# Down projection of the channel mixer: three groups of k tiles by Strassen's seven products, two weight sums made by loads that accumulate

## The chip, the cores and the metric

One core of one Trainium2 chip. The metric is the device time of one execution in microseconds (us), the median over runs. Engines: PE (TensorE, matrix products; PEld is its weight load), DVE (VectorE), ACT (ScalarE), POOL (GpSimd), SP (SyncE, which here only issues transfers). Each engine has its own queue and runs it in order; between engines there are semaphores.

## The reference

Four layers over 512 tokens of 1024 channels in float32. Each layer is a token mixer (convolution module, 2-D neighbourhood attention, bidirectional retention, convolution module again), then a channel mixer. Each of the two reads the RMS-normed residual and adds its result to it.

```python
for i in range(DEPTH):                       # 4
    ...                                      # token mixer, x = x + y
    h = rmsnorm(x, norm2_g[i])
    x = x + conv_ffn(h, ffn_w_up[i], ffn_dw_w[i], ffn_dw_b[i], ffn_w_down[i])
```

`conv_ffn` multiplies by `w_up` (1024 x 5632), applies a depthwise convolution of width 3 over the tokens, takes the tanh form of gelu of one half times the other half (2816 hidden channels), and multiplies by `w_down` (2816 x 1024). The change concerns this last product.

## The kernel before

Everything lies transposed: channels on the 128 partitions, 512 tokens (T) in the free dimension. The residual is eight tiles x0 to x7. A float32 product is made of three products in the faster float32r form: every operand is split into a rounded high half and a low half (the difference), and `mm3` (L161 to L164) issues hi x hi, hi x lo and lo x hi into the same PSUM bank. A weight tile arrives by one load on SP's queue into `wr` (two buffers of 1024 columns); ACT casts it to `wh` (L157), DVE subtracts to get `wl` (L158). Three buffers each of `wh` and `wl` let the split run ahead of PE.

`ffn(l, after)` runs the channel mixer of layer l. `up(n)` makes one of 44 column blocks of the up projection (8 input tiles x 3 products of 128x512). `mid(j)` takes two of those, applies the convolution and the gate (DVE L298, L303, L305, L309; ACT L301, L308), and splits the result into `hh` and `hl` (L172, L173), for 22 hidden tiles j. Then a loop over the eight output tiles o loads three pieces of weights (1024, 896, 896 columns), runs 22 k tiles x 3 products of 128x512 into one bank, adds the bank to x[o] (`residual`, L274), and calls `after(o)`. In layers 0 to 2 `after(o)` is `prep` of the next stage: `xh` (ACT L229), `xl` (DVE L232), a square (ACT L245) and its addition to `sqacc` (POOL L250). In layer 3 it is the store of x[o] (L1044); there the last output tile is made in two token halves with an addition (L362) and a store each.

The order on each engine is made by the Tile scheduler from the program's order, its priorities and its own model of durations; the kernel does not write it out.

## Time and profile before

| what | value |
|---|---|
| median of 3 runs | 2581.75 us (2581.56 to 2582.65) |
| profiled execution: span from first to last instruction | 2576.2 us, the time of that execution as the profile has it |
| granted TensorE clock | 1.000 |
| PE rows in the program's order | 13168 |

A row of the timeline reads: start in us, length in us, engine, line, operation, out<-in, shapes, and in brackets the idle time before it with what ended it. A row by groups reads: line, engine, operation, out<-in, shapes, count, then busy us and mean ns of one, then idle time before it and what ended it. In the row on a window of time the engines stand in the order PE, PEld, DVE, ACT, POOL with their busy us, then the granted clock, the DMA engines' busy share and GB/s. A row of transfers has the issuing queue (SPq, POOLq), the count, KB each, and the median us from issue to landing.

### The profile page before, as it was taken

What the parts mean: (1) busy time and instruction counts of PE and PEld (TensorE: products, weight loads), DVE (VectorE), ACT (ScalarE), POOL (GpSimd) and SP (SyncE); (2) the same over time, 40 slices, a digit from 0 to 9 for tenths busy, and PEclk for the clock granted to TensorE, in tenths of its full rate; (3) what the DMA queues carried; (4) which work ended last, traced back from release to release, by engine and by line L of the source; (5) the groups of instructions that cost most, each with busy time, mean ns of one, the idle gap of its engine ahead of it and who ended that gap; (6) DMA issues with size and microseconds to landing.
All of it is one profiled execution on the core that took longest, in us unless ns stands there. A gap on an engine that the chain in (4) does not pass through costs nothing.

```text
span 2576.2 us, 33719 instructions
## 1 busy us (share of the span) xinstructions
PE 2558.8 (99%) x13414; PEld 2120.2 (82%) x13414; DVE 1652.3 (64%) x2673; ACT 1050.0 (41%) x1439; POOL 258.8 (10%) x301
## 2 busy tenths in 40 slices
PE   9999999999999999999999999999999999999999
PEld 7878888889998888888888888888888888788888
DVE  7986777338877777624656566677743787677732
ACT  5554444335556444423333323444432445444421
POOL 1213000003421100000000000100000221100000
PEclk9999999999999999999999999999999999999999
DMA  6724232333332322233222221232333672222232
GB/s 241 234 86 148 90 98 88 95 103 105 97 91 71 101 95 95 90 97 110 74 85 71 84 80 58 98 99 90 97 90 97 206 222 74 90 93 95 92 107 80
DMA packets 80174, 271.78 MB, mean 105 GB/s; under 512 B 10720, under 2 KB 13664, under 8 KB 80016
## 3 DMA queue, kind: packets, MB, share of 16 engines
q1 hardware_dynamic: 73152, 256.32, 30.9%
q0 software_dynamic: 5568, 10.59, 1.7%
q10 hardware_dynamic: 1296, 2.72, 0.3%
q8 instruction: 105, 1.72, 0.3%
q14 instruction: 53, 0.43, 0.1%
HBM read 260.19 MB, written 5.63 MB: 103 GB/s over the span
## 4 chain that ended last, share of the span: by engine, by line
PE 97%; DVE 2%; ACT 0%; issue 0%; DMA 0%; SPq 0%; DVEq 0%; ACTq 0%
PE ps L164 27%; PE ps L163 27%; PE ps L162 27%; PE ps L168 3%; PE ps L169 3%; PE ps L167 3%; PE ps L485 1%; PE ps L484 1%; PE ps L483 1%; PE ps L332 1%; PE ps L333 1%; PE ps L337 1%; PE ps L724 1%; DMA x<-in_xT 0%; PE ps L539 0%
## 5 line engine op out<-in xcount | busy, mean ns | idle before, releaser
L157 ACT CAST wh<-wr 128x1024 fp32r<-128x1024 f32 (+1 forms) x410 | 423.1, 1033 | 1086.1 <-PE ps L163 775.9
L164 PE MATMUL ps<-xh,wl 128*128 128x512 f32 x1856 | 735.4, 397 | 0.1
L163 PE MATMUL ps<-xl,wh 128*128 128x512 f32 x1856 | 734.5, 396 | 0.2 <-DVE xl L232 0.2
L162 PE MATMUL ps<-xh,wh 128*128 128x512 f32 x1856 | 730.4, 394 | 0.4 <-ACT wh L157 0.4
L158 DVE TENSOR_TENSOR wl<-wr,wh 128x1024 fp32r<-128x1024 f32 (+1 forms) x407 | 494.9, 1216 | 334.4 <-ACT wh L157 332.1
L162 PEld LDWEIGHTS ps<-xh,wh 128*128 128x128 f32 x1856 | 348.5, 188 | 85.8 <-ACT wh L157 1.3
L163 PEld LDWEIGHTS ps<-xl,wh 128*128 128x128 f32 x1856 | 348.4, 188 | 85.9 <-DVE xl L232 0.5
L164 PEld LDWEIGHTS ps<-xh,wl 128*128 128x128 f32 x1856 | 348.3, 188 | 81.7 <-DVE wl L158 0.5
L162 PE MATMUL ps<-hh,wh 128*128 128x512 f32 (+1 forms) x726 | 281.6, 388 | 0.5 <-DVE x L362 0.5
L163 PE MATMUL ps<-hl,wh 128*128 128x512 f32 (+1 forms) x726 | 281.5, 388 | 0.0
L164 PE MATMUL ps<-hh,wl 128*128 128x512 f32 (+1 forms) x726 | 281.5, 388 | 0.0
L298 DVE TENSOR_TENSOR t<-ps,rstd_bc 128x512 f32<-128x512 f32 x176 | 120.8, 690 | 159.1 <-PE ps L164 159.1
L250 POOL TENSOR_TENSOR sqacc<-t,sqacc 128x512 f32<-128x512 f32 x49 | 75.1, 1533 | 1253.6 <-ACT t L245 1248.2
L162 PEld LDWEIGHTS ps<-hh,wh 128*128 128x128 f32 x726 | 136.6, 188 | 31.0 <-DVE x L362 0.7
L163 PEld LDWEIGHTS ps<-hl,wh 128*128 128x128 f32 x726 | 136.7, 188 | 30.3
L164 PEld LDWEIGHTS ps<-hh,wl 128*128 128x128 f32 x726 | 136.7, 188 | 30.3
L168 PE MATMUL ps<-wl,xh 128*128 128x256 f32 (+1 forms) x512 | 159.1, 312 | 0.5 <-DVE wl L158 0.5
L169 PE MATMUL ps<-wh,xl 128*128 128x256 f32 (+1 forms) x512 | 159.1, 312 | 0.0
L167 PE MATMUL ps<-wh,xh 128*128 128x256 f32 (+1 forms) x512 | 158.4, 312 | 0.0
L301 ACT ACTIVATE t<-t,par 128x512 f32<-128x512 f32 x176 | 142.5, 814 | 6.0 <-DVE t L298 5.8
L305 DVE SCALAR_TENSOR_TENSOR t<-t,par,t 128x511 f32<-128x511 f32 x176 | 132.0, 750 | 5.5
L303 DVE SCALAR_TENSOR_TENSOR t<-t,par,t 128x511 f32<-128x511 f32 x176 | 130.8, 744 | 0.0
(256 smaller groups left out, 3572.4 us busy)
## 6 DMA issues: line engine op xcount, KB each, us to landing
wr<-in_f_up SPq DMA_DIRECT2D x176, 512.0 KB, 3.4
wraw<-in_cdw SPq DMA_DIRECT2D x56, 608.0 KB, 5.1
wr<-in_f_down SPq DMA_DIRECT2D x64, 448.0 KB, 3.3
wr<-in_f_down SPq DMA_DIRECT2D x32, 512.0 KB, 3.5
wr<-in_cw_in SPq DMA_DIRECT2D x30, 512.0 KB, 3.9
wr<-in_nat_qkv SPq DMA_DIRECT2D x24, 512.0 KB, 3.5
wr<-in_cw_out SPq DMA_DIRECT2D x16, 512.0 KB, 3.9
wr<-in_ret_qk SPq DMA_DIRECT2D x16, 512.0 KB, 3.5
```

The costliest lines, as they stand in the source:

```text
L157: nc.scalar.copy(hi[:, :n], raw[:, :n])
L158: eng.tensor_tensor(lo[:, :n], raw[:, :n], hi[:, :n].bitcast(F32), SUB)
L162: nc.tensor.matmul(o, wh, ah, start=first, stop=False)
L163: nc.tensor.matmul(o, wh, al, start=False, stop=False)
L164: nc.tensor.matmul(o, wl, ah, start=False, stop=last)
L167: nc.tensor.matmul(o, ah, wh, start=first, stop=False)
L168: nc.tensor.matmul(o, ah, wl, start=False, stop=False)
L169: nc.tensor.matmul(o, al, wh, start=False, stop=last)
L298: nc.vector.tensor_tensor(u, ps, rstd_bc, MUL)
L301: nc.scalar.activation(a, u, AF.Identity, bias=pc("fdb", l * 44 + c), scale=pt[:, w + 1:w + 2])
L303: nc.vector.scalar_tensor_tensor(a[:, 1:], u[:, :T - 1], pt[:, w:w + 1], a[:, 1:], MUL, ADD)
L305: nc.vector.scalar_tensor_tensor(a[:, :T - 1], u[:, 1:], pt[:, w + 2:w + 3], a[:, :T - 1], MUL, ADD)
```

## The change

The first 20 of the 22 k tiles are taken as ten pairs, cut into three groups (`PARTS`): four, three and three pairs. For each group, the weights are a matrix of 2 x 2 blocks (even or odd k tile of a pair, output tile 2i or 2i+1), and the hidden vectors are 2 x 2 blocks too (even or odd k tile, first or second half of the tokens). The product of the two is made by Strassen's seven products in Winograd's form, each of 128x256, instead of eight. `down(q)` runs group q for the four output pairs i; `weights(i, q)` makes the weight operands and `mid` the seven hidden operands.

- Weights, per i and group, with n = 512 columns in the first group and 384 in the others: one load of two blocks (`wr`, 2n columns, split at L166 and L167), a load of block a21 into `wt` and one into `ws3` (L386, L387), onto which POOL issues a load each that accumulates a22 and a11 in place (L388, L389), and a load of a12 into `wq` (L396). Then DVE adds a11 to make the second half of `wt` (L398), `wt` is split (L167), `ws3` is split (`h3`, `l3`, L403), DVE adds `wq` (L404) and that is split (`h4`, `l4`, L408). In the last group the two k tiles left over have their own weights (`r5`, `h5`, `l5`, L182).
- Hidden operands: `mid` writes the gated product of two j into `F` (one buffer), POOL makes four half-width additions (L333, L335, L336, L337), ACT casts the seven blocks (L341, L342), DVE subtracts (L343, L345) into `Hh` and `Hl` (four slots).
- Results, per i: ACT copies two partial sums out of PSUM into `s12`, POOL adds x[2i+1] (L464), DVE takes `u2` out of PSUM (L473), POOL adds it to x[2i] (L476; DVE for the last i of the last group), DVE adds x[2i+1] (L448). In the last group 2 k tiles x 3 products of 128x512 for each output tile follow in `remainder`, added by DVE (L283 for x[2i], L440 for `s12`), and `after` is called for both tiles.
- Order in the program: group 0 stands after the up projections of j = 8, group 1 after those of j = 14, group 2 after all. The weights of a group's first output pair come before the last `mid` that the group needs, and a group's last two products come after the next two up products (`filler`). The temporary pool shrinks from 9 to 7 tiles, and the weights lie in another order in memory.

PE's rows grow from 13168 to 14542. The following pieces are from the programs' orders, layer 0; numbers behind a name tell one buffer from another.

PE before, at the border of two output tiles: `ps631` is the bank of x2, `ps642` that of x3.

```order
L162 MATMUL ps631_4463<-hh608_4279,wh639_4478 128x512
L163 MATMUL ps631_4463<-hl609_4280,wh639_4478 128x512
L164 MATMUL ps631_4463<-hh608_4279,wl640_4479 128x512
L162 MATMUL ps642_4554<-hh318_2630,wh644_4557 128x512 [waits Activation_49]
L163 MATMUL ps642_4554<-hl319_2631,wh644_4557 128x512
L164 MATMUL ps642_4554<-hh318_2630,wl645_4558 128x512 [waits DVE_49]
```

PE after, in the final group: `ps818` is a bank of the fourth output pair (i = 3), `ps795` the one of the third, whose last products take `h4` and `l4`.

```order
L171 MATMUL ps818_5613<-Hh714_5117,wh809_5594 128x256
L172 MATMUL ps818_5613<-Hl715_5118,wh809_5594 128x256
L173 MATMUL ps818_5613<-Hh714_5117,wl810_5595 128x256
L171 MATMUL ps795_5479<-Hh660_4791,h4789_5468 128x256 [waits DVE_49]
L172 MATMUL ps795_5479<-Hl661_4792,h4789_5468 128x256
L173 MATMUL ps795_5479<-Hh660_4791,l4790_5469 128x256
```

Before, one output tile's products run to the end before the next one's; now products of two output pairs take turns, and the last two of a pair come after the first four of the next.

DVE before, at the end of layer 0's channel mixer: three weight splits for each addition of an output tile and each low half for the next stage.

```order
L158 TENSOR_TENSOR wl645_4558<-wr643_4555,wh644_4557 128x1024 [waits DMAHW0_49,PE_49,Activation_49]
L158 TENSOR_TENSOR wl648_4564<-wr646_4561,wh647_4563 128x896 [waits DMAHW1_49,PE_49,Activation_49]
L274 TENSOR_TENSOR x2_81<-ps631_4463,x2_81 128x512 [waits PE_49]
L158 TENSOR_TENSOR wl651_4570<-wr649_4567,wh650_4569 128x896 [waits DMAHW2_49,Activation_49]
L232 SCALAR_TENSOR_TENSOR xl2_97<-x2_81,png_104,xh2_89 128x8x64 [waits Activation_49]
```

DVE after, the same place in the final group: `wl847` and `wl850` are weights of the next stage, `l4790` belongs to the third output pair, `l5817` to the fourth, `t796` is `s12` of the third.

```order
L167 TENSOR_TENSOR wl847_5795<-wr845_5792,wh846_5794 128x1024 [waits DMAHW6_49,PE_49,Activation_49]
L283 TENSOR_TENSOR x2_81<-ps797_5520,x2_81 128x512 [waits Pool_49]
L241 SCALAR_TENSOR_TENSOR xl2_97<-x2_81,png_104,xh2_89 128x8x64 [waits Activation_49]
L167 TENSOR_TENSOR wl850_5801<-wr848_5798,wh849_5800 128x1024 [waits DMAHW1_49,PE_49,Activation_49]
L448 TENSOR_TENSOR x3_82<-ps772_5346,t773_5347 128x512 [waits PE_49]
L408 TENSOR_TENSOR l4790_5469<-wq782_5452,h4789_5468 128x768 [waits Activation_49]
L440 TENSOR_TENSOR t796_5480<-ps823_5668,t796_5480 128x512 [waits PE_49,Pool_49]
L182 TENSOR_TENSOR l5817_5609<-r5815_5607,h5816_5608 128x512 [waits DMAHW3_49,Activation_49]
```

Splits that PE needs soon now stand behind additions that wait for PE and for POOL.

POOL before, at the same place: only the sums of squares.

```order
L250 TENSOR_TENSOR sqacc_107<-t630_4460,sqacc_107 128x512 [waits PE_49,Activation_49]
L250 TENSOR_TENSOR sqacc_107<-t641_4551,sqacc_107 128x512 [waits Activation_49,Pool_49]
L250 TENSOR_TENSOR sqacc_107<-t652_4642,sqacc_107 128x512 [waits Activation_49,Pool_49]
L250 TENSOR_TENSOR sqacc_107<-t663_4733,sqacc_107 128x512 [waits Activation_49,Pool_49]
L250 TENSOR_TENSOR sqacc_107<-t674_4824,sqacc_107 128x512 [waits Activation_49,Pool_49]
```

POOL after:

```order
L464 TENSOR_TENSOR t753_5257<-x1_80,t753_5257 128x512 [waits Activation_49]
L476 TENSOR_TENSOR x0_79<-x0_79,t755_5308 128x512 [waits DVE_49]
L389 DMA ws3805_5582<-in_f_down 128x384 [waits DMAHW7_49,DMASW4_49,Activation_49]
L464 TENSOR_TENSOR t773_5347<-x3_82,t773_5347 128x512 [waits Activation_49]
L259 TENSOR_TENSOR sqacc_107<-t776_5427,sqacc_107 128x512 [waits PE_49,Activation_49]
L476 TENSOR_TENSOR x2_81<-x2_81,t778_5441 128x512 [waits DVE_49]
L259 TENSOR_TENSOR sqacc_107<-t798_5530,sqacc_107 128x512 [waits Activation_49,Pool_49]
L464 TENSOR_TENSOR t796_5480<-x5_84,t796_5480 128x512 [waits Activation_49]
```

The sums of squares (L259 now) alternate with additions to the residual and issues of accumulating loads, each waiting for another engine.

The diff, without `mm3` (which only gets a flag), and without a branch that `DMA_SUMS` leaves unused:

```diff
+PARTS = ((0, 4), (4, 7), (7, 10))
+PART_COL = (0, 2048, 3584, 5120)
+REST = 20
+SLOT_H = 4
+NF = 1
+NT_FFN = 7
+NWT = 2
+NWQ = 1
+DMA_SUMS = True
...
 
     def ffn(l, after):
         with ExitStack() as st:
-            stage_pools(st, 9, 8, 0)
+            stage_pools(st, NT_FFN, 8, 0)
             hp = st.enter_context(tc.tile_pool(name=nm("ffn"), bufs=1, reuse_waits=RW))
-            hh, hl = [], []
+
...
+            H, rest, cur_f = {}, {}, {}
 
             def mid(j, pv, pg):
...
                 nc.scalar.activation(acc[1], acc[1], AF.Gelu_apprx_tanh)
-                nc.vector.tensor_tensor(acc[0], acc[0], acc[1], MUL)
-                hi = hp.tile([P, T], F32R, tag=f"hh{j}", name=nm("hh"))
-                lo = hp.tile([P, T], F32R, tag=f"hl{j}", name=nm("hl"))
-                split(acc[0], hi, lo)
-                hh.append(hi)
-                hl.append(lo)
+                if j >= REST:
+                    nc.vector.tensor_tensor(acc[0], acc[0], acc[1], MUL)
+                    hi = hp.tile([P, T], F32R, tag=f"rh{j}", name=nm("hh"))
+                    lo = hp.tile([P, T], F32R, tag=f"rl{j}", name=nm("hl"))
+                    split(acc[0], hi, lo)
+                    rest[j] = (hi, lo)
+                    return
+                if j % 2 == 0:
+                    cur_f["F"] = hp.tile([P, 8, 256], F32, tag="F", name=nm("F"), bufs=NF)
+                F, b = cur_f["F"], 2 * (j % 2)
+                nc.vector.tensor_tensor(F[:, b:b + 2, :].rearrange("p a b -> p (a b)"), acc[0], acc[1], MUL)
+                gp = nc.gpsimd.tensor_tensor
+                if j % 2 == 0:
+                    gp(F[:, 4, :], F[:, 1, :], F[:, 0, :], SUB)
+                    return
+                gp(F[:, 7, :], F[:, 2, :], F[:, 4, :], ADD)
+                gp(F[:, 5, :], F[:, 2, :], F[:, 0, :], SUB)
+                gp(F[:, 6, :], F[:, 7, :], F[:, 3, :], SUB)
+                sl = (j // 2) % SLOT_H
+                hi = hp.tile([P, 7, 256], F32R, tag=f"Hh{sl}", name=nm("Hh"))
+                lo = hp.tile([P, 7, 256], F32R, tag=f"Hl{sl}", name=nm("Hl"))
+                nc.scalar.activation(hi[:, 6, :], F[:, 7, :], AF.Copy, scale=-1.0)
+                nc.scalar.copy(hi[:, :6, :], F[:, 1:7, :])
+                nc.vector.scalar_tensor_tensor(
+                    lo[:, 6, :], F[:, 7, :], -1.0, hi[:, 6, :].bitcast(F32), MUL, SUB)
+                nc.vector.tensor_tensor(lo[:, :6, :], F[:, 1:7, :], hi[:, :6, :].bitcast(F32), SUB)
+                H[j // 2] = (hi, lo)
...
-            ups, done = up_first(), 0
-            for n in range(1, 2 * FT):
-                if n > 1:
-                    ups.append(up(n))
-                while n >= S2[l] and done < len(ups) // 2:
+            def weights(i, q):
+                p0, p1 = PARTS[q]
+                n, c = (p1 - p0) * P, PART_COL[q]
+                src = f_down[l, i]
+                r1 = load_raw(src[:, c:c + 2 * n], 2 * n)
+                t = hp.tile([P, D], F32, tag="wt", name=nm("wt"), bufs=NWT)
+                s3 = hp.tile([P, T], F32, tag="ws3", name=nm("ws3"), bufs=2)
+                a11, a22 = slice(c, c + n), slice(c + n, c + 2 * n)
+                a21, a12 = slice(c + 2 * n, c + 3 * n), slice(c + 3 * n, c + 4 * n)
+                if DMA_SUMS:
+                    nc.sync.dma_start(t[:, :n], src[:, a21])
+                    nc.sync.dma_start(s3[:, :n], src[:, a21])
+                    nc.gpsimd.dma_start(t[:, :n], src[:, a22], accum_op=ADD)
+                    nc.gpsimd.dma_start(s3[:, :n], src[:, a11], accum_op=ADD)
...
+                sg = hp.tile([P, D], F32, tag="wq", name=nm("wq"), bufs=NWQ)
+                nc.sync.dma_start(sg[:, n:2 * n], src[:, a12])
+                w1 = split_w(r1, 2 * n, nc.vector)
+                nc.vector.tensor_tensor(t[:, n:2 * n], t[:, :n], r1[:, :n], ADD)
+                w2 = split_w(t, 2 * n, nc.vector)
+                h3 = hp.tile([P, T], F32R, tag="h3", name=nm("h3"))
+                l3 = hp.tile([P, T], F32R, tag="l3", name=nm("l3"))
+                nc.scalar.copy(h3[:, :n], s3[:, :n])
+                nc.vector.tensor_tensor(l3[:, :n], s3[:, :n], h3[:, :n].bitcast(F32), SUB)
+                nc.vector.tensor_tensor(sg[:, :n], t[:, n:2 * n], sg[:, n:2 * n], ADD)
+                h4 = hp.tile([P, D], F32R, tag="h4", name=nm("h4"))
+                l4 = hp.tile([P, D], F32R, tag="l4", name=nm("l4"))
+                nc.scalar.copy(h4[:, :2 * n], sg[:, :2 * n])
+                nc.vector.tensor_tensor(l4[:, :2 * n], sg[:, :2 * n], h4[:, :2 * n].bitcast(F32), SUB)
+                lastw = None
+                if q == len(PARTS) - 1:
+                    r5 = hp.tile([P, T], F32, tag="r5", name=nm("r5"))
+                    h5 = hp.tile([P, T], F32R, tag="h5", name=nm("h5"))
+                    l5 = hp.tile([P, T], F32R, tag="l5", name=nm("l5"))
+                    nc.sync.dma_start(r5, src[:, PART_COL[-1]:])
+                    split(r5, h5, l5)
+                    lastw = (h5, l5)
+                u = lambda w, b: (w[0][:, b * n:(b + 1) * n], w[1][:, b * n:(b + 1) * n])
+                return {"a11": u(w1, 0), "a22": u(w1, 1), "s1": u(w2, 0), "s2": u(w2, 1),
+                        "s3": u((h3, l3), 0), "sg": u((h4, l4), 0), "a12": u((h4, l4), 1), "rest": lastw}
+
+            def prod(o, w, q, b, start, stop=True):
+                p0, p1 = PARTS[q]
+                for p in range(p0, p1):
+                    s = slice((p - p0) * P, (p - p0 + 1) * P)
+                    hi, lo = H[p]
+                    mm3(o, w[0][:, s], w[1][:, s], hi[:, b, :], lo[:, b, :],
+                        start and p == p0, stop and p == p1 - 1, True)
+
+            def down(q, first=None, filler=None):
+                final = q == len(PARTS) - 1
+
+                def remainder(i, w, s12):
+                    for o, h in ((2 * i, 0), (2 * i + 1, 2)):
+                        ps = bank(psa)
+                        for k in range(REST, FT):
+                            s = slice((h + k - REST) * P, (h + k - REST + 1) * P)
+                            mm3(ps, w["rest"][0][:, s], w["rest"][1][:, s], *rest[k],
+                                k == REST, k == FT - 1)
+                        if h:
+                            nc.vector.tensor_tensor(s12, ps, s12, ADD)
+                        else:
+                            residual(o, ps)
+                            after(o)
+
+                def tail(i, w, v, s12):
+                    prod(v[:, :256], w["sg"], q, 1, False)
+                    prod(v[:, 256:], w["a12"], q, 2, True)
+                    nc.vector.tensor_tensor(x[2 * i + 1], v, s12, ADD)
+                    if final:
+                        after(2 * i + 1)
+
+                prev = None
+                for i in range(4):
+                    w = first if i == 0 and first else weights(i, q)
+                    xb, v = bank(psa), bank(psa)
+                    xc = xb[:, :256]
+                    s12 = t512()
+                    prod(xc, w["a11"], q, 0, True)
+                    nc.scalar.copy(s12[:, 256:], xc)
+                    prod(v[:, 256:], w["a22"], q, 5, True)
+                    prod(v[:, :256], w["s1"], q, 3, True)
+                    prod(xc, w["s2"], q, 6, False)
+                    nc.scalar.copy(s12[:, :256], xc)
+                    nc.gpsimd.tensor_tensor(s12, x[2 * i + 1], s12, ADD)
+                    if prev:
+                        if final:
+                            remainder(prev[0], prev[1], prev[3])
+                        tail(*prev)
+                    prod(xc, w["s3"], q, 4, False)
+                    s3 = hp.tile([P, 256], F32, tag="sn3", name=nm("sn3"), bufs=2)
+                    nc.scalar.activation(s3, xc, AF.Copy, scale=-1.0)
+                    u2 = t512()
+                    nc.vector.tensor_tensor(
+                        u2.rearrange("p (h t) -> p h t", h=2), s3.unsqueeze(1).broadcast_to([P, 2, 256]),
+                        v.rearrange("p (h t) -> p h t", h=2), SUB)
+                    (nc.vector if final and i == 3 else nc.gpsimd).tensor_tensor(
+                        x[2 * i], x[2 * i], u2, ADD)
+                    prev = (i, w, v, s12)
+                if final:
+                    remainder(prev[0], prev[1], prev[3])
+                if filler:
+                    filler()
+                tail(*prev)
+
+            ups = up_first()
+            done, n = 0, 2
+
...
-            for o in range(KD):
...
+            for j in range(1, FT):
+                ups_of(j)
+                if n > S2[l]:
+                    mids(j)
+                for q, (_, p1) in enumerate(PARTS[:-1]):
+                    if j == 2 * p1:
+                        w0 = weights(0, q)
+                        mids(j + 1)
+                        down(q, w0, lambda: ups_of(j + 1))
+            w0 = weights(0, len(PARTS) - 1)
+            mids(FT)
+            down(len(PARTS) - 1, w0)
```

More of the change, by code (lines that the diff above doesn't have):

```diff
@@ L159, in split_w, with mm3 @@
         return hi, lo
-    def mm3(o, wh, wl, ah, al, first, last):
-        nc.tensor.matmul(o, wh, ah, start=first, stop=False)
-        nc.tensor.matmul(o, wh, al, start=False, stop=False)
-        nc.tensor.matmul(o, wl, ah, start=False, stop=last)
+    def mm3(o, wh, wl, ah, al, first, last, free=False):
+        nc.tensor.matmul(o, wh, ah, start=first, stop=False, skip_group_check=free)
+        nc.tensor.matmul(o, wh, al, start=False, stop=False, skip_group_check=free)
+        nc.tensor.matmul(o, wl, ah, start=False, stop=last, skip_group_check=free)
     def mm3s(o, wh, wl, ah, al, first, last):
@@ L342, in up_first @@
                 return pss
[L344 to L348 removed]
+            def weights(i, q):
[13 more added lines that the diff above has]
+                else:
+                    r21 = hp.tile([P, T], F32, tag="r21", name=nm("r21"))
+                    nc.sync.dma_start(r21[:, :n], src[:, a21])
+                    nc.gpsimd.tensor_tensor(t[:, :n], r21[:, :n], r1[:, n:2 * n], ADD)
+                    nc.gpsimd.tensor_tensor(s3[:, :n], r21[:, :n], r1[:, :n], ADD)
+                sg = hp.tile([P, D], F32, tag="wq", name=nm("wq"), bufs=NWQ)
[23 more added lines that the diff above has]
+                        "s3": u((h3, l3), 0), "sg": u((h4, l4), 0), "a12": u((h4, l4), 1), "rest": lastw}
@@ L349, in ffn, with mids @@
+            ups = up_first()
+            done, n = 0, 2
+            def mids(upto):
+                nonlocal done
+                while done < upto:
                     mid(done, ups[2 * done], ups[2 * done + 1])
                     done += 1
[L351 to L368 removed]
@@ new lines, in ups_of @@
+            def ups_of(j):
+                nonlocal n
+                while n < 2 * j + 2:
+                    ups.append(up(n))
+                    n += 1
+            for j in range(1, FT):
[7 more added lines that the diff above has]
+                        down(q, w0, lambda: ups_of(j + 1))
@@ L1171, in _layout @@
     rout = f["ret_w_out"][0].reshape(4, 4, P, 4, 2, P).transpose(0, 3, 2, 4, 1, 5)
+    fd = f["ffn_w_down"].reshape(4, FT, P, 8, P)
+    macros = []
+    for i in range(4):
+        units = [fd[:, 2 * p0 + par:2 * p1:2, :, o] for p0, p1 in PARTS
+                 for o, par in ((2 * i + 1, 0), (2 * i, 1), (2 * i, 0), (2 * i + 1, 1))]
+        units += [fd[:, REST:, :, o] for o in (2 * i, 2 * i + 1)]
+        macros.append(np.concatenate(
+            [u.transpose(0, 2, 1, 3).reshape(4, P, -1) for u in units], -1))
+    fdown = np.stack(macros, 1)
     arrays = {
@@ L1190, in _layout @@
         "f_up": tiles(f["ffn_w_up"]),
-        "f_down": tiles(f["ffn_w_down"]),
+        "f_down": fdown,
     }
```

20 lines of the change are left out of this document (2 added, 18 removed).

## Prediction

> **What bounds the kernel now.** I read the page first: how busy each engine is, and what the chain that ended last consists of.
>
> ```profile
> span 2576.2 us, 33719 instructions
> PE 2558.8 (99%) x13414; PEld 2120.2 (82%) x13414; DVE 1652.3 (64%) x2673; ACT 1050.0 (41%) x1439; POOL 258.8 (10%) x301
> PEclk9999999999999999999999999999999999999999
> PE 97%; DVE 2%; ACT 0%; issue 0%; DMA 0%; SPq 0%; DVEq 0%; ACTq 0%
> ```
>
> PE (TensorE) is busy for 99% of the span at the full granted clock, and 97% of the chain is PE. So the time is the number of matmuls times their pace, as long as nobody makes PE wait. Second I looked at how the down projection runs. The view of one tile (the hi half of the hidden vector) in layer 0, and the engines' busy time over the same stretch:
>
> ```profile
> L162 PE MATMUL ps<-hh,wh x176: 392/394/398, 453.8 to 576.3; 128*128 128x512 f32 x176
> L164 PE MATMUL ps<-hh,wl x176: 392/395/398, 454.3 to 576.8; 128*128 128x512 f32 x176
> 440.00:580.00 140.00, 140.00 (x614) 113.16 (x614) 56.84 (x58) 50.01 (x50) 8.01 (x6) 1.00 0.33 98
> ```
>
> From the first product at 453.8 to the last at 576.8 lie 527 starts, 123.0 us, 0.2334 each; PE is busy for all 140 us of the window, while DVE (VectorE) works 56.84, ACT (ScalarE) 50.01, POOL (GpSimd) 8.01 and the DMA engines are a third busy. The stage has no gaps to win; it has idle time on the other engines to spend. Third, the pace itself, from the timeline: of 512-wide products in the middle of layer 3's down projection, and of 256-wide ones in its last row block, which is already computed in two halves.
>
> ```profile
> 2499.61 0.40 PE L162 MATMUL ps<-hh,wh 128*128 128x512 f32 x1
> ...
> 2507.97 0.40 PE L162 MATMUL ps<-hh,wh 128*128 128x512 f32 x1
> ...
> 2557.73 0.28 PE L164 MATMUL ps<-hh,wl 128*128 128x256 f32 x1
> ...
> 2563.79 0.28 PE L164 MATMUL ps<-hh,wl 128*128 128x256 f32 x1
> 2564.58 0.39 PE L162 MATMUL ps<-hh,wh 128*128 128x256 f32 x1 [0.52 <-DVE x L362]
> L164 PEld LDWEIGHTS ps<-hh,wl 128*128 128x128 f32 x32 | 6.0, 188 | 0.0
> ```
>
> Between the first two rows lie 36 starts: 8.36 / 36 = 0.2322 us. Between the next two lie 51: 6.06 / 51 = 0.1188 us. Half the width costs half the time (0.512 of it), although each half-width product still has its own weight load, which lasts 188 ns and overlaps its neighbours. This decides whether seven half-size products can be cheaper than eight.
>
> **The change, part by part.** *Products.* A layer's down projection has 22 k tiles x 8 output tiles x 3 = 528 products of 512, 528 x 0.2322 = 122.6 us. After it, 7 products x 10 k pairs x 4 output pairs x 3 = 840 of 256 and, for the two k tiles left over, 2 x 8 x 3 = 48 of 512: 840 x 0.1188 + 48 x 0.2322 = 99.8 + 11.1 = 110.9. That is -11.7 a layer, -46.6 for four. The halves of the last row block vanish: 132 x 0.1188 = 15.7 instead of 66 x 0.2322 = 15.3, and a start that came 0.79 after its predecessor instead of 0.12 (the row with the wait for DVE), together -1.0. PE term: **-47.6 us**, none of it hidden, since PE is the chain.
>
> *What DVE, ACT and POOL get.* Prices, grouped by line and shape:
>
> ```profile
> L158 DVE TENSOR_TENSOR wl<-wr,wh 128x1024 fp32r<-128x1024 f32 x343 | 425.0, 1239 | 232.9 <-ACT wh L157 232.4
> L305 DVE SCALAR_TENSOR_TENSOR t<-t,par,t 128x511 f32<-128x511 f32 x176 | 132.0, 750 | 5.5
> L298 DVE TENSOR_TENSOR t<-ps,rstd_bc 128x512 f32<-128x512 f32 x176 | 120.8, 690 | 159.1 <-PE ps L164 159.1
> L309 DVE TENSOR_TENSOR t<-t,t 128x512 f32<-128x512 f32 x88 | 60.9, 692 | 58.7 <-ACT t L308 58.7
> L232 DVE SCALAR_TENSOR_TENSOR xl<-x,png,xh 128x512 fp32r<-128x512 f32 x64 | 63.2, 999 | 8.1 <-ACT xh L229 7.9
> L173 DVE TENSOR_TENSOR hl<-t,hh 128x512 fp32r<-128x512 f32 x88 | 60.2, 684 | 2.7 <-ACT hh L172 2.7
> L274 DVE TENSOR_TENSOR x<-ps,x 128x512 f32<-128x512 f32 x55 | 38.0, 691 | 122.2 <-PE ps L164 122.2
> L250 POOL TENSOR_TENSOR sqacc<-t,sqacc 128x512 f32<-128x512 f32 x49 | 75.1, 1533 | 1253.6 <-ACT t L245 1248.2
> L686 POOL TENSOR_TENSOR bm<-W,mask 128x256 f32<-128x256 f32 x48 | 39.7, 855 | 34.8 <-DVE sm L711 28.8 <-issue 5.5 <-DMA mask<-in_nmask 0.2
> ```
>
> DVE's slope is (1239 - 684) / 512 = 1.084 ns an element, so 768 wide is 0.96 us and 384 wide 0.545. In groups of three pairs, one output pair costs DVE three splits of 768 (2.88), three operations of 384 (1.64), and, in the final group, the remainder's split (0.68), two low halves of the next stage's input (2 x 0.75) and four additions out of PSUM (4 x 0.69): 6.7 us with two SBUF inputs and 2.8 us out of PSUM, 9.5 in all. POOL gets two full-width additions, beside two squares of the next stage; at 1.3 (below) that is 5.2 us. PE needs 63 x 0.1188 + 12 x 0.2322 = 10.3 us. Each engine alone fits, so the question is whether DVE and POOL run side by side. The timeline of the end of layer 0's convolution mixer says what happens when they meet:
>
> ```profile
> 196.47 2.41 POOL L158 TENSOR_TENSOR wl<-wr,wh 128x1024 fp32r<-128x1024 f32 x1 [2.15 <-ACT wh L157]
> 197.05 2.38 DVE L232 SCALAR_TENSOR_TENSOR xl<-x,png,xh 128x512 fp32r<-128x512 f32 x1 [0.83 <-ACT xh L229]
> 203.16 0.75 DVE L232 SCALAR_TENSOR_TENSOR xl<-x,png,xh 128x512 fp32r<-128x512 f32 x1
> 203.28 1.78 POOL L250 TENSOR_TENSOR sqacc<-t,sqacc 128x512 f32<-128x512 f32 x1 [2.71 <-ACT t L245]
> 182.79 1.33 POOL L250 TENSOR_TENSOR sqacc<-t,sqacc 128x512 f32<-128x512 f32 x1 [43.20 <-ACT t L245]
> 184.94 1.42 POOL L250 TENSOR_TENSOR sqacc<-t,sqacc 128x512 f32<-128x512 f32 x1 [0.81 <-ACT t L245]
> 185.13 0.68 DVE L554 TENSOR_TENSOR x<-ps,x 128x512 f32<-128x512 f32 x1
> ```
>
> A DVE operation of 0.75 us that starts while POOL works ends 0.55 after POOL's end (2.38 us instead of 0.75), and POOL's addition, 1.33 when alone, takes 1.78 behind a DVE one. The addition out of PSUM at 185.13 keeps its 0.68 beside POOL. So operations with two SBUF inputs exclude POOL's, and those out of PSUM don't.
>
> The Trainium skill says the same more strictly ("SBUF — State Buffer", section "Who interferes with whom"): the port pair that DVE and GpSimd share is an exclusive lock for a whole instruction, a DVE instruction with two SBUF inputs contends with a GpSimd one that reads SBUF, and one with at most one SBUF input doesn't. The rows agree; by the rule the final group's term below would be 19.5 us instead of 15.
>
> *Final group, layers 0 to 2.* Fully exclusive, an output pair needs 6.7 + 5.2 = 11.9 us against PE's 10.3: 1.6 x 4 = 6.5 a layer. I also stepped the two queues along PE's order at the paces above, from the final group's first weights. PE ends the last product of output pair i = 1 29.4 us in; only then can DVE add x3 (0.69), split l4 of i = 2 (0.96), add the remainder (0.69) and split l5 of i = 3 (0.68): ready at 32.4, and PE asks for it at 32.8. With two POOL operations in between it is 2.2 (1.3 each) to 3.2 us late (1.78 each). Later DVE splits a weight of the next stage (1.24) that waits for a buffer which PE releases at 35.8, and behind it stand xl4, x5, the remainder and l4 of i = 3, 3.1 us: ready at 40.1 where PE asks at 39.2, 0.9 late, 2.2 to 2.7 with one POOL operation. The sum is 0.9 without contention, 4.4 to 5.9 with it; I take **5 a layer, +15**, since the blocked row is the nearest one. Bounds 0 (both covered) and 8 (6.5 and one more split of 1.24), so 0 to 24. In layer 3 stores take the place of the next stage's inputs and squares: 0 to 1.
>
> *Groups 0 and 1* stand in the middle of the up projections, and their products alternate with those of the up projections, which keeps most deadlines 0.8 us or more behind what is due. New there: POOL's four half-width additions per pair of j (4 x 0.855 = 3.4 us), and a load that adds to what lies in SBUF, issued by POOL. No row shows an adding load; the nearest:
>
> ```profile
> wr<-in_f_down SPq DMA_DIRECT2D x64, 448.0 KB, 3.3
> x<-in_xT SPq DMA_DIRECT2D x8, 256.0 KB, 4.3
> xf<-u POOLq DMA_DIRECT2D x112, 34.0 KB, 3.8
> wd<-gp POOLq DMA_DIRECT2D x16, 192.0 KB, 5.5
> L435 POOL DMA_DIRECT2D xf<-u x112 | 58.4, 566 | 205.8 <-DVE u L431 115.5 <-issue 55.4 <-DVE yd L444 23.2
> ```
>
> Issue to landing is 3.8 to 5.5 us for POOL's loads, 3.3 to 4.3 for SP's, and an issue holds POOL for 0.57. DVE's sum t + r1 waits for it in queue order; behind it stand the next splits, and PE waits for those. Up to about 5 us it lands in time. In POOL's queue these loads stand between the additions, and one behind an addition that waits for a product of PE is issued later by about that product, 1 us. The pieces that are loaded grow from four to seven for each output pair; the DMA engines, a third busy, have room. I take 5, the middle of POOL's rows, and +0.75 a group (one load in each of them late by less than a product) for eight groups, **+6**; bounds 0, and 3 a group (two operations held up by a POOL operation of 1.5), 24. A gain is excluded in these terms, since PE's own count stands in the first.
>
> The Trainium skill has a price ("DMA: Bandwidth & Descriptors", section "Anatomy of one DMA — SWDGE (gpsimd) path"): about 2.0 us plus the bytes at 436 GB/s, for 256 KB an estimate of 2.6 us, by which this term would be some 2 us smaller. No run here shows an adding load, and its rows for POOL's loads are all longer.
>
> *Up projections.* Per pair of j DVE has four splits of 1.24, four muls of 0.69, eight of 0.75, two products of 0.69 and low halves of 1536 and 256, 2.2 by the slope: 17.3 us, and POOL 3.4: 20.7 of PE's 96 x 0.2322 = 22.3 even when fully exclusive. Two weights are split ahead, so 0; without that cover it would be one blocked operation, 1.3, at each pair.
>
> *Transitions and end.* The last two input tiles of the next stage now come from one output pair, 0.7 later, three times; the end adds and stores 512 columns instead of 256:
>
> ```profile
> 2572.72 0.42 DVE L362 TENSOR_TENSOR x<-ps,x 128x256 f32<-128x256 f32 x1 [8.20 <-PE ps L164]
> out<-x SPq DMA_DIRECT2D x7, 256.0 KB, 2.0
> out<-x SPq DMA_DIRECT2D x2, 128.0 KB, 1.7
> ```
>
> 0.69 - 0.42 + 2.0 - 1.7 = 0.6. With the layer 3 allowance it makes **+3** (0 to 6).
>
> **Sum.** -47.6 + 15 + 6 + 3 = -23.6: the span 2576.2 becomes 2552.6. The span lies 5.55 below the median of the runs, 2581.75; with the same 5.5 outside it the time is **2558**. With all terms at their lower bounds 2534, at their upper 2588.
>
> **Rivals.** *The covers hold.* DVE alone fits in every stretch, and if POOL's operations happen to fall beside PSUM additions, a final group loses 1 to 2 us: -47.6 + 5 + 1 + 1 = -40.6, 2541 (2536 to 2548). Against it: the 2.38 us row.
>
> *The exclusion binds in all three groups.* 6.5 x 3 = 19.5 and 2.6 x 8 = 21: -47.6 + 19.5 + 21 + 3 = -4, 2578 (2572 to 2587). For it: POOL works 4 half-width additions and 2 full ones where it had almost nothing. Against: up products lie between.
>
> *The adding load is slow* (the other side). It must read, add and write what an ordinary load only writes. If it needs much more than 5 us, PE stalls by the excess at one to three sums a group, 8 to 24 in all. My sum turns slower by 0.2% when 28.8 us come on top, 3.6 at each of 8 sums: from 8.6 us a load, or 7.4 with 12 sums. At 10 us it is +40 to +120, say 2600 at the least. Against it: no load in the rows above takes more than 5.5 us.
>
> *Half the width doesn't halve the time,* because the weight load of 188 ns sets the pace: 840 x 0.188 + 11 = 169 a layer, +46, 2770. The 51 intervals of 0.1188 exclude it nearly.
>
> **Chances.** 0.2%, 5.2 us, is about what a measurement of this kernel tells from no change. Forecast, 2548 to 2572: 0.52. Covers hold: 0.15. Exclusion everywhere: 0.15, of which 0.09 lie within 0.2% (2576.6 to 2586.9) and 0.06 below. Slow adding load: 0.15. Half-width pace: 0.01. Below 2536: 0.02. So faster 0.52 + 0.15 + 0.06 + 0.02 = 0.75, same 0.09, slower 0.16. The range 2538 to 2587 holds the forecast, nearly all of the case below and the exclusion, 0.80.
>
> **What would show it.** Right: 256-wide products 0.119 apart; the down work's PE waits named DVE l4, l5 and remainder, 4 to 6 us in each of the first three final groups; DVE operations of 2 us and more beside POOL's; groups 0 and 1 almost gapless; the adding loads landing after 4 to 5.5 us. Wrong: PE waits behind t + r1 or ws3 with a DMA as the releaser; gaps at the first product of a group (hidden vectors late); PE waits in the up projections on wl; or a final group as dense as the stage is now.

## The result, and the profile after

The changed kernel is slower: 2604.93 us (2600.51 to 2609.96, 4 runs) against 2582.2 (4 runs), ratio 1.0089, interval 1.0074 to 1.0104. The forecast was 2558, with 2538 to 2587 as its range. From the page of the changed kernel, and from the view of its cores:

```profile
span 2608.2 us, 38020 instructions
PE 2544.1 (98%) x14788; PEld 2176.2 (83%) x14788; DVE 1933.9 (74%) x2980; ACT 1185.0 (45%) x1695; POOL 649.7 (25%) x649
PE 72%; DVE 9%; DMA 5%; issue 2%; ACT 2%; POOL 1%; DVEq 0%; SPq 0%; POOLq 0%; ACTq 0%
```

```profile
core 0: 2608.2 us, clock 0.990
```

PE still reads 98% busy, but its share of the chain fell from 97 to 72%, and the mean granted clock from 1.000 to 0.990. What PE waited for (engine, line, whom; us in all, times, longest):

```profile
PE ps L171 <- DVE t L473: 12.3, 4, 4.2
PE ps L173 <- DVE wl L167: 10.6, 8, 1.8
PE ps L218 <- DVE rstd_col L267: 9.5, 3, 3.7
PE ps L173 <- DVE l L182: 5.9, 3, 2.5
PE ps L171 <- ACT t L463: 3.7, 3, 1.8
```

All waits of PE sum to 59 us, against 14 in the kernel before. The account of the profiled execution, whose span is 32.0 longer:

| term | forecast | measured |
|---|---|---|
| products | -47.6 | about -41: the 256-wide products start 0.1207 apart in the mean at full clock, where the prediction took 0.1188 |
| waits in the final groups (u2, l5, L463, one of 0.6) | +16 | +22.5 |
| waits in and ahead of groups 0 and 1, and of the final group's first weights | +6 | +12.6 |
| waits for rstd_col and sqacc at the start of the channel mixer | 0 | +10.5 |
| transitions and end | +2 | +1 |
| half clock | 0 | about +21 |

The rows sum to about +27; some 5 us are not assigned. The half clock is worked out so: (1 - 0.990) x 2608.2 is 26, but in those stretches PE is busy for only 46.5 of 51 us (the rest is counted as waits), and its products there start 0.213 us apart instead of 0.119, 1.8 times as slowly and not twice. The two largest differences from the forecast, the half clock and the start of the channel mixer, had no term at all.

**The clock.** Windows of the first final group's end, in the columns of the earlier row of windows (the clock stands third from the end), and two of 1 us:

```profile
584.00:587.41 3.41, 0.59 (x5) 0.39 (x4) 3.41 (x5) 3.26 (x5) 1.42 (x1) 1.00 0.38 105
587.41:590.83 3.42, 2.06 (x9) 2.06 (x10) 3.39 (x5) 1.45 (x2) 1.83 (x1) 0.50 0.13 52
590.83:594.24 3.41, 3.41 (x18) 3.41 (x17) 2.07 (x3) 2.21 (x2) 1.45 (x2) 0.50 0.06 10
594.24:597.65 3.41, 3.41 (x31) 3.41 (x30) 1.90 (x3) 2.42 (x2) 1.40 (x2) 1.00 0.71 221
136.00:137.00 1.00, 1.00 (x19) 1.00 (x18) 1.00 (x2) 0.59 (x1) 0.00 (x0) 0.93 0.00 0
2253.00:2254.00 1.00, 0.04 (x1) 0.04 (x1) 0.77 (x5) 0.00 (x0) 0.28 (x1) 0.56 1.11 361
```

PE is busy for only 0.59 and then 2.06 us of the first two windows (the cell that begins at 587.41 is itself at half clock); each is followed by 3.41 us at half clock, in which a full window holds 18 products (all 256 wide) instead of 31. A row of 1 us at clock c begins its half clock 2 x (1 - c) from its end: 136.86 and 2253.12 in the last two rows. All twelve beginnings in this execution lie on one grid, 20.80 plus a multiple of 3.4133 us, within 0.02. So a wait that leaves PE idle for much of one cell of this grid costs its length and up to 1.5 us more for each cell that follows at half clock (3.41 us with starts 0.213 apart instead of 0.119). The Trainium skill ("TensorE: Matmul & The Clock Gate", section "Part 1: The HAM clock gate (the "warmup" mystery)") has this window, free-running, 4096 cycles or 3413 ns, with half clock after an idle one; the grid agrees. A wholly idle cell isn't needed, though: every cell here with 1.9 us or more of idle PE was followed by half clock. Below that it went either way: cells with 1.28, 1.60, 1.76 and 1.78 us were followed by it, those with 1.67, 1.69 and 1.81 were not, so idle time alone doesn't give the limit. Two of the twelve beginnings, at 136.86 and 150.51, stand behind waits that the kernel before has as well; its profiled execution has no half clock, but other runs of it show mean clocks of 0.997 to 0.999.

**The final group.** DVE and PE at the end of layer 1's, in order of time:

```profile
1202.02 1.52 DVE L167 TENSOR_TENSOR wl<-wr,wh 128x1024 fp32r<-128x1024 f32 x1 [0.70 <-ACT wh L166]
1204.07 1.44 DVE L408 TENSOR_TENSOR l<-wq,h 128x768 fp32r<-128x768 f32 x1
1206.03 1.35 DVE L182 TENSOR_TENSOR l<-r,h 128x512 fp32r<-128x512 f32 x1
1207.43 0.50 PE L173 MATMUL ps<-hh,l 128*128 128x512 f32 x1 [2.50 <-DVE l L182]
1213.08 1.23 DVE L167 TENSOR_TENSOR wl<-wr,wh 128x1024 fp32r<-128x1024 f32 x1 [1.64 <-ACT wh L166]
1214.22 1.78 DVE L241 SCALAR_TENSOR_TENSOR xl<-x,png,xh 128x512 fp32r<-128x512 f32 x1
1217.99 0.67 DVE L473 TENSOR_TENSOR t<-sn,ps 128x512 f32<-128x512 f32 x1
1218.72 0.46 PE L171 MATMUL ps<-Hh,h 128*128 128x256 f32 x1 [3.31 <-DVE t L473]
```

This is the chain that the prediction stepped: splits of the next stage's weights wait for buffers, and l5 and then u2 stand behind them. L182 takes 1.35 instead of 0.68, L408 1.44 instead of 0.96, L241 1.78 instead of 0.75, beside POOL.

### The profile page after: what moved, and what is told of

Read it like the earlier page. It is cut to its first block, busy times and chain, and to the rows that moved or that the text cites. A ratio compares the mean times of both kernels' runs of the same rounds, so it can differ in the third digit from the quotient of the medians.

```text
span 2608.2 us, 38020 instructions
## 1 busy us (share of the span) xinstructions
PE 2544.1 (98%) x14788; PEld 2176.2 (83%) x14788; DVE 1933.9 (74%) x2980; ACT 1185.0 (45%) x1695; POOL 649.7 (25%) x649
## 4 chain that ended last, share of the span: by engine, by line
PE 72%; DVE 9%; DMA 5%; issue 2%; ACT 2%; POOL 1%; DVEq 0%; SPq 0%; POOLq 0%; ACTq 0%
PE ps L171 20%; PE ps L173 20%; PE ps L172 20%; DVE wl L167 3%; PE ps L176 3%; PE ps L178 3%; PE ps L177 3%; DMA wt<-in_f_down 3%; DMA wr<-in_f_down 2%; ACT wh L166 1%; DVE t L314 1%; DVE t L316 1%; DVE Hl L345 1%; DVE xl L241 1%; PE ps L628 1%
## 5 line engine op out<-in xcount | busy, mean ns | idle before, releaser
L171 PE MATMUL ps<-xh,wh 128*128 128x512 f32 x1856 | 740.5, 400 | 1.2 <-ACT wh L166 1.2
L166 ACT CAST wh<-wr 128x1024 fp32r<-128x1024 f32 (+1 forms) x362 | 372.7, 1030 | 656.4 <-PE ps L172 429.3
L167 DVE TENSOR_TENSOR wl<-wr,wh 128x1024 fp32r<-128x1024 f32 (+1 forms) x359 | 448.9, 1251 | 132.4 <-ACT wh L166 131.8
L173 PE MATMUL ps<-Hh,wl 128*128 128x256 f32 x640 | 176.7, 285 | 10.6 <-DVE wl L167 10.6
L172 PE MATMUL ps<-Hl,wh 128*128 128x256 f32 x640 | 180.4, 284 | 2.1 <-DVE Hl L345 1.5
L171 PE MATMUL ps<-Hh,wh 128*128 128x256 f32 x640 | 178.0, 284 | 0.4 <-ACT wh L166 0.4
L171 PE MATMUL ps<-Hh,h 128*128 128x256 f32 x480 | 139.4, 291 | 16.2 <-DVE t L473 12.3
L316 DVE SCALAR_TENSOR_TENSOR t<-t,par,t 128x511 f32<-128x511 f32 x176 | 141.3, 807 | 3.6
L314 DVE SCALAR_TENSOR_TENSOR t<-t,par,t 128x511 f32<-128x511 f32 x176 | 138.9, 794 | 0.0
L172 PE MATMUL ps<-Hl,h 128*128 128x256 f32 x480 | 138.5, 289 | 0.0
L173 PE MATMUL ps<-Hh,l 128*128 128x256 f32 x480 | 138.4, 288 | 0.0
L259 POOL TENSOR_TENSOR sqacc<-t,sqacc 128x512 f32<-128x512 f32 x49 | 75.5, 1541 | 245.4 <-ACT t L254 244.9
```

The lines of the kernel that those rows point to most:

```text
L166: nc.scalar.copy(hi[:, :n], raw[:, :n])
L167: eng.tensor_tensor(lo[:, :n], raw[:, :n], hi[:, :n].bitcast(F32), SUB)
L171: nc.tensor.matmul(o, wh, ah, start=first, stop=False, skip_group_check=free)
L172: nc.tensor.matmul(o, wh, al, start=False, stop=False, skip_group_check=free)
L173: nc.tensor.matmul(o, wl, ah, start=False, stop=last, skip_group_check=free)
L314: nc.vector.scalar_tensor_tensor(a[:, 1:], u[:, :T - 1], pt[:, w:w + 1], a[:, 1:], MUL, ADD)
```

## The experiments

Each is read against the kernel before on the same chip (median 2578.9 to 2579.6 there); the changed kernel stands at +0.89%, 23 us. Gains are differences of these ratios, each known to about 4 us, so a gain is known to some 5 us. The diffs are shortened.

**1. Operands behind the norm statistics.**

```diff
+ state["rcol"] = nc.vector.tensor_copy(rstd_col, r);  state["rbc"] = nc.scalar.copy(rstd_bc, ps)
+ def weights(i, q):
+     with behind("rcol", "rbc"): return weights_(i, q)      # weights_: the function as it was
```

> Edit: the operands of all weights() calls (ACT casts, DVE splits and sums) are queued behind the end of the norm statistics (rstd_col on DVE, rstd_bc on ACT); nothing else. Theory A (queue order at the start of the channel mixer): the splits l3 and l5 and the wl that waits behind them no longer stand inside the small-operation chain of the reciprocal root, so the chain takes about 5.2 us from reduction to rstd_col as in the kernel before, not 8.7; the three waits of PE for rstd_col (3.74, 2.92, 2.83 us) go, and with them the half clock that follows: 9.5 us of waits and up to 4 windows of half clock worth 1.7 us each, so 2605 becomes 2589 to 2596. Rival: the operands come too late for group 0 instead, and the waits move there: within 4 us of 2605.

2591.07, ratio 1.0042 (1.0025 to 1.0059): 12 us gained. DVE in layer 0 of the changed kernel, then of this one, first and last of the chain:

```profile
224.11 0.68 DVE L213 TENSOR_REDUCE sm<-ps 128x4 f32<-128x512 f32 x1
226.59 0.69 DVE L403 TENSOR_TENSOR l<-ws,h 128x512 fp32r<-128x512 f32 x1 [0.59 <-ACT h L402]
231.66 1.23 DVE L167 TENSOR_TENSOR wl<-wr,wh 128x1024 fp32r<-128x1024 f32 x1 [0.74 <-ACT wh L166]
232.80 0.16 DVE L267 COPY rstd_col<-sm 128x4 f32<-128x4 f32 x1
```

```profile
219.65 0.69 DVE L213 TENSOR_REDUCE sm<-ps 128x4 f32<-128x512 f32 x1 [8.85 <-PE ps L211]
224.86 0.17 DVE L267 COPY rstd_col<-sm 128x4 f32<-128x4 f32 x1
```

The chain took 8.7 us with a split of group 0 (L403) and weight splits that waited inside it, and 5.2 with two weight splits that did not wait. PE's waits for rstd_col are gone, and the time is in the range of theory A, which holds.

**2. The next stage's weights later.**

```diff
+ # second and third weight tile of the next stage:
+ with behind("mark", "markA"): ...   # mark: u2 (L473) of the last output pair
```

> Edit: of the next stage's first three weight tiles, the second and third are cast and split only after the final group's last u2 (L473) on DVE and the copy before it on ACT. Theory A (queue order in the final group): DVE no longer stands behind a split that waits for a buffer of PE, so in layers 0 to 2 PE's waits for l5 (0.9, 2.5, 2.5 us), for u2 (4.2, 3.3, 3.4) and for the copy L463 (1.8, 1.2, 0.8) fall from 20.6 us to 6 or less, and most of 7 windows of half clock go (1.7 us each): gain 15 to 25, 2580 to 2590. Rival 1 (DVE and POOL exclude each other and are full): the waits stay above 12 us in sum and the gain is under 8. Rival 2: the next stage's first products wait 1 to 3 us for their weights, three times, and eat up to 9 of it.

2593.67, ratio 1.0061 (1.0044 to 1.0079): 7 us gained. PE's waits; lines are 8 higher here:

```profile
PE ps L226 <- DVE rstd_col L275: 10.3, 3, 5.0
PE ps L179 <- DVE t L481: 6.0, 4, 1.9
PE ps L181 <- DVE l L190: 5.1, 4, 1.9
PE ps L179 <- ACT h L189: 4.7, 4, 2.0
```

The waits for u2 halved, as A has it; in their place came waits for `h5` on ACT (4.7) and nearly all of those for l5 stayed. With 1.2 for L463 the final groups' waits are 17.0 instead of 22.5: an order was at fault, but not this one alone. Both signs of rival 1 came out (waits above 12 us, gain under 8); run 7 tries its mechanism by itself. At the start of the next stage PE waited 3.1 us instead of 0.4, which is rival 2, at a third of its price.

**3. A third buffer for wt.**

```diff
- NWT = 2
+ NWT = 3        # and sn3: bufs=2 -> bufs=1
```

> Edit: three buffers for wt instead of two (and one for the small sn3 instead of two, for room). Theory A (two loads in series: a plain one of 3.1 us, then the accumulating one of 4.6, begun only when a buffer of wt comes free): the sum t + r1 waits less for its load (3 to 4.5 us of DVE idle at some 10 places), and PE's waits for wl of 1 to 1.9 us at 10 places (12 us) fall to 3 or less; with the half clock behind one or two of them the gain is 8 to 13, 2592 to 2597. Rival (the accumulating load is late for another reason, such as its place in POOL's queue): the waits stay, within 4 us of 2605.

2603.19, ratio 1.0090 (1.0075 to 1.0105): nothing gained. Yet the mechanism was there. The accumulating loads in the changed kernel's list of transfers:

```profile
wt<-in_f_down POOLq DMA_DIRECT2D x32, 192.0 KB, 4.7
ws<-in_f_down POOLq DMA_DIRECT2D x32, 192.0 KB, 5.4
```

One late sum and its price, from its timeline, all queues in order of time:

```profile
543.01 0.33 SPq L386 DMA_DIRECT2D wt<-in_f_down  x1
546.54 0.87 POOL L388 DMA_DIRECT2D wt<-in_f_down  x1 [9.34 <-DVE wl L167]
551.20 0.56 DVE L398 TENSOR_TENSOR wt<-wt,wr 128x384 f32<-128x384 f32 x1 [4.51 <-DMA wt<-in_f_down]
552.68 0.39 PE L173 MATMUL ps<-Hh,wl 128*128 128x256 f32 x1 [1.78 <-DVE wl L167]
```

DVE's sums by groups, the idle time ahead of them last: the changed kernel, then this one.

```profile
L398 DVE TENSOR_TENSOR wt<-wt,wr 128x384 f32<-128x384 f32 x32 | 20.4, 636 | 50.6 <-DMA wt<-in_f_down 41.6 <-DMA wr<-in_f_down 9.1
```

```profile
L398 DVE TENSOR_TENSOR wt<-wt,wr 128x384 f32<-128x384 f32 x32 | 21.8, 682 | 26.6 <-DMA wr<-in_f_down 26.6
```

PE's waits with three buffers:

```profile
PE ps L173 <- DVE wl L167: 0.7, 1, 0.7
PE ps L171 <- DVE t L473: 17.1, 6, 5.2
PE ps L218 <- DVE rstd_col L267: 13.1, 3, 5.8
```

From the first load's issue to the sum lie 8.2 us, two loads in series: the plain one landed at 545.98, the accumulating one at 551.17. (The row of 546.54 names a split on DVE, which ended 0.1 us after that landing.) With a third buffer no sum waits for the accumulating load any more, and PE's waits for wl fall from 10.6 to 0.7; the waits for u2 and rstd_col grow by 4.8 and 3.6. The rival named the time, not the cause. Why those waits grew is not shown.

**4. No accumulating loads.**

```diff
- DMA_SUMS = True
+ DMA_SUMS = False   # POOL adds: wt = r21 + a22, ws3 = r21 + a11
```

> Edit: no accumulating loads; a21 is loaded once and POOL makes both sums (two additions of 384 or 512 columns more for each output pair and group). Theory A (the accumulating load costs by its series of two loads, and POOL's additions cost by excluding DVE): the waits for wl at 10 places go (12 us), POOL gets 96 additions of about 1 us, which stretch DVE operations by up to 0.6 each; the final groups lose 1 to 3 us each: between 8 faster and 10 slower, 2597 to 2615. Rival (the loads cost nothing, all is exclusion): 15 or more slower, above 2620.

2642.98, ratio 1.0246 (1.0230 to 1.0261): 40 us slower than the changed kernel, the rival's side. One group of POOL's new additions, and two of PE's waits:

```profile
L393 POOL TENSOR_TENSOR wt<-r,wr 128x384 f32<-128x384 f32 x32 | 36.5, 1142 | 154.4 <-DMA wr<-in_f_down 154.4
```

```profile
PE ps L171 <- ACT wh L166: 15.6, 6, 4.2
PE ps L172 <- DVE hl L182: 10.0, 8, 1.5
```

With 96 more POOL additions of 1.1 us and more, PE waits for splits and casts in every group, at a clock of 0.988. The loads cost less than what they replace; that the exclusion alone makes the difference is not shown.

**5 and 6. Waits of a known length, in the kernel before.**

```diff
+ # output tiles 1 to 7 of layers 0 to 2; hz is hh[0] at first; m = 1 or 3
+ for b in range(m):
+     z = hp.tile([P, T], F32R, tag=f"hz{b}", name=nm("hz"))
+     nc.vector.scalar_tensor_tensor(z, prev, 0.0, hz.bitcast(F32), MUL, ADD)    # prev: bank of the tile before
+     hz = z
```

> The kernel before with 21 waits put into it: ahead of output tiles 1 to 7 of the down projection in layers 0 to 2, one DVE operation of 0.7 us makes the first hidden operand (its value unchanged) from the finished bank of the tile before, and PE waits for it. Theory A (a wait of PE costs its own length while it leaves PE busy for half of a window of 3.41 us, and halves the clock for the next window when it doesn't): each wait is about 1.2 us, the granted clock stays 1.000, +21 x 1.2 = +25, 2605. Rival (any wait can drop the clock): clock 0.99 or less and +40 or more.

> The same with three DVE operations in a row, so that each of the 21 waits is about 2.5 us. Theory A: 21 x 2.5 = +53 from the waits; a wait of 2.5 us fills more than half of one window of 3.41 us in 7 of 10 places on the grid, so about 15 windows of half clock follow, 1.7 us each, +26: 2660, granted clock about 0.99, and every stretch of half clock begins at a multiple of 3.413 us apart. Rival (the lower clock of the changed kernel has nothing to do with the waits): clock 1.000 and 2633.

The view of the cores and PE's waits on the new operation, first with one operation, then with three:

```profile
core 0: 2613.6 us, clock 0.999
```

```profile
PE ps L162 <- DVE hz L357: 25.0, 17, 1.5
```

```profile
core 0: 2724.2 us, clock 0.979
```

```profile
PE ps L162 <- DVE hz L357: 98.6, 21, 4.7
```

With one operation each of 21 waits was 1.47 us (four are booked to a neighbour), longer than the 1.2 expected, 30.9 in all; not one was followed by half clock, and the time rose by 36.8 to 2616.0, of which some 6 are not accounted for. With three it was 4.7, longer than the 2.5 expected; all 21 were followed by one or two cells of half clock, and the time rose by 146 to 2725.0: 99 of waits and about 45 of clock. Waits three times as long cost four times as much. On the clock theory A holds against both rivals; by time the first run lies nearer its rival's +40 than the +25 of theory A, without the rival's lower clock. The share of 7 in 10 could not be tried at this length.

**7. POOL narrow in the final group.** POOL's additions there take 8 of 512 columns; the rest of those sums is left out.

```diff
- nc.gpsimd.tensor_tensor(s12, x[2 * i + 1], s12, ADD)      # likewise L476, and L259 in prep
+ nc.gpsimd.tensor_tensor(s12[:, :8], x[2 * i + 1][:, :8], s12[:, :8], ADD)
```

> The changed kernel with POOL's operations of the final group (both additions to the residual, and the additions of squares for the next stage) cut to 8 of 512 columns; what they would have added is left out. Theory A (DVE and POOL exclude each other): DVE's operations with two SBUF inputs go back to their own length (L182 0.69 instead of 1.2 to 1.4, L408 0.96 instead of 1.45), nobody waits for POOL, and PE's waits in the final groups of layers 0 to 2 (20.6 us) fall to 8 or less, with the half clock behind them 12 to 25 faster: 2580 to 2593. Rival (queue order: splits of the next stage wait for buffers that PE frees, whatever POOL does): the waits stay above 14 and the gain is under 8.

2591.83, ratio 1.0049 (1.0034 to 1.0064): 10 us gained. The split of l5 by groups in the changed kernel, the same here, and PE's waits here:

```profile
L182 DVE TENSOR_TENSOR l<-r,h 128x512 fp32r<-128x512 f32 x16 | 19.1, 1193 | 26.6 <-ACT h L181 26.6
```

```profile
L182 DVE TENSOR_TENSOR l<-r,h 128x512 fp32r<-128x512 f32 x16 | 12.3, 770 | 27.6 <-ACT h L181 27.6
```

```profile
PE ps L171 <- DVE t L475: 10.6, 4, 3.1
PE ps L173 <- DVE l L182: 2.8, 3, 1.2
PE ps L171 <- ACT t L464: 2.3, 4, 1.6
```

The exclusion is real (1.19 to 0.77 us for l5), but of the 20.6 us of waits in layers 0 to 2 only 6.3 go with it: 14.3 stay, just over the rival's 14 (the rows above have 1.45 of layer 3 besides). The gain lies between the two theories, whose bounds were 12 and 8. The larger part of the waits does not need POOL; that it is the order of DVE's queue is argued from runs 2 and 9, where a new order alone halved the waits for u2.

**8 to 10. The edits together.** First 1 to 3, then also the low halves and squares of x4 and x5 behind the last u2, with three and with two buffers for wt:

```diff
+ # prep of the next stage, from the last output pair's iteration on:
+ state["defer"].append(low); state["defer"].append(squares)    # run behind "mark"
```

> The three edits together: operands behind the norm statistics, the next stage's second and third weights behind the final group's last u2, three buffers for wt. Theory A (they remove separate waits): the gains add, 13.9 + 11.3 and the waits for wl of the remaining order (6.8 us): 2572 to 2580, as fast as before or a little faster. Rival (each edit lets the scheduler move other waits into the places): 2585 or more.

> The three edits, and the low halves (DVE L241 in the changed kernel) and squares (ACT, POOL) of x4 and x5 are queued behind the last u2 of the final group in layers 0 to 2. Where the three edits left it: PE waits 5.5, 5.2 and 5.2 us for that u2, since xl4 (1.75 us beside POOL's square) and xl5 (2.15) stand ahead of it. Theory A (a queue holds what PE needs behind what it doesn't): these three waits fall from 15.9 to 4 or less, and six or seven windows of half clock behind them (1.7 us each) to one or two: 2584 becomes 2562 to 2570, faster than the kernel before by 0.4 to 0.7%. Rival (DVE is full in the final group): the waits move to l4, x7 or the next stage's start, 2578 or more.

> The same with two buffers for wt. Theory A (each sum t + r1 that is late for its two loads in series costs PE 1 to 1.9 us, at 5 to 10 places): 6 to 12 slower than with three buffers. Rival (what the third buffer removed comes back elsewhere, as it did alone): within 3 us.

Edits 1 to 3: 2584.3, ratio 1.0021 (1.0012 to 1.0030), 17 us better than the changed kernel, between theory A (up to 2580) and the rival (from 2585). The largest wait left was for u2, with xl4 and, in the row below, xl5 ahead of it in the queue (PE's waits, then DVE's timeline at the end of layer 0):

```profile
PE ps L179 <- DVE t L485: 20.1, 6, 5.5
```

```profile
581.32 2.15 DVE L249 SCALAR_TENSOR_TENSOR xl<-x,png,xh 128x512 fp32r<-128x512 f32 x1
583.40 0.67 DVE L485 TENSOR_TENSOR t<-sn,ps 128x512 f32<-128x512 f32 x1
```

With xl4 and xl5 deferred: 2576.89, ratio 0.9991 (0.9981 to 1.0000), 25 us better than the changed kernel and level with the one before. The waits for u2 fell from 20.1 to 9.9 us; the three behind xl5 went from 15.9 to 5.7, not to 4, and PE waited 4.7 us at the start of the next stages, as the rival had it. The time is 7 above theory A's range and 1 below the rival's; the profiled clock is 0.994. With two buffers it is 2591.96, 1.0047 (1.0034 to 1.0060): here the third buffer is worth 15 us, more than the 6 to 12 expected, where alone it was worth nothing.

**11 and 12. PE's order.**

```diff
+ with behind("pe"): remainder(last pair)        # after its s3 product; 12: every pair's, after s2
```

> As the run before with all edits (2577), and the remainder's 12 products of 512 columns (2.8 us) of the last output pair queued on PE between the last s3 product and the last pair's tail, instead of ahead of s3. There PE waited 1.8 to 1.95 us for u2 (product, copy on ACT, subtraction on DVE in series) in layers 0 to 2, with half clock behind each. Theory A (PE's own order leaves nothing to do while u2 is made): these waits go, 5.7 us, and three windows of half clock, 1.7 us each: 2566 to 2571, 0.3 to 0.5% faster than the kernel before. Rival (DVE, late by itself, then makes PE wait for l5 or the next tail just as long): 2575 or more.

> The same for every output pair of the final group: the remainder of pair i - 1 is queued on PE behind the s2 product of pair i, and the last one as in the run beside it. Theory A: the waits of 1.3 to 1.45 us for u2 of the earlier pairs shrink too, 2 to 6 faster than the run beside it. Rival (the products that now come earlier wait for their weights instead): slower than it by 2 or more.

2582.46, 1.0012 (1.0003 to 1.0021), and 2590.43, 1.0039 (1.0025 to 1.0052). In the first the wait ahead of the last tail is gone, but PE waits 7.2 us at the start of the next stages, where it waited 4.7, and 2.9 for L463 in layer 0. In the second it waits 11.0 for u2, 6.8 for the copy L459 and 9.8 at the start of the next stages. The times are those of both rivals; the waits are not the ones that these named (l5 or the tail, and weights). No version that beats the kernel before was found.

## Why the prediction was wrong

The forecast was 24 us faster, and 23 slower was measured. In the prediction's own terms:

- *Products, -47.6.* The count was right; the pace was a little too good. 51 starts of one quiet stretch gave 0.1188 us; the 3360 products of this kernel start 0.1207 apart in the mean where no wait lies between, and the term measures about -41.
- *What bounds the kernel.* The step "the time is the number of matmuls times their pace, as long as nobody makes PE wait" failed where waits were added to it: each was priced at its own length. The half clock behind waits is about 21 us, the difference between a forecast of 2558 and 2579 with nothing else changed. The profile of before could not show its price: its waits were 1.93 us at most, and its clock 1.000.
- *Final group, +15 and 0 to 1 in layer 3.* The places (l5, and the last pair behind a split for the next stage) were right; the size was 6.8, 7.0 and 6.7 a layer instead of 5, and 2.0 in layer 3. The last wait was booked to u2 rather than l4, one place further on in the same queue. The step that failed is the stepping without contention, 0.9 a layer: with POOL narrow (run 7) 14.3 us stay in three layers, 4.8 each. So the exclusion was given most of the term and has about a third of it, and that the sum came as near as it did is partly luck.
- *Groups 0 and 1, +6.* The adding loads landed as assumed in the median, 4.7 to 5.7 (single ones 3.5 to 9.5). The step that failed is "Up to about 5 us it lands in time": it counted one load where two stand in series, 8.2 us to the sum (run 3). Measured 12.6, of which 10.6 are the waits for wl that the third buffer takes away. What POOL's half-width additions cost in these groups, no run tried.
- *Start of the channel mixer, 0.* A term that was missing. Groups' operands were counted in their groups, but the scheduler had hoisted them to the stage's start, into the chain of the norm; 10.5 us, which run 1 removed.
- *The slow rival* named loads of over 7.4 us; in the median the load was no slower than POOL's others, and the kernel lost time without it. The exclusion in all groups, up to 2587, had almost the measured sum of waits (43.5 against 45.6) and was still too fast a case, for want of the clock.
- The 5.5 us outside the span were too many: runs here whose span is 2576.2 took 2578.0. The forecast had taken the span of one execution from the median of others.

## What to carry to other kernels

Where PE is full, price a wait by what it does to the clock, not only by its length: 21 waits of 1.47 us cost 37, 21 of 4.7 cost 146. When work moves from the full engine to the others, follow each one's queue order to the first thing that PE needs behind something it doesn't, also at the far end of the stage to which a scheduler may hoist it. A saving of products is worth only what the order of the queues leaves of it; here four edits together brought back 25 us, which made the kernel level with the one before; the 41 us of saved products still went into waits and clock.
